# A hybrid streaming-encoder step: a margin in the planner that orders TensorE, and two groups of loads asked for at other places

## The chip, the cores and the metric

One NeuronCore of one Trainium2 chip runs the whole step. The metric is the device time of one execution in microseconds, lower is better. A kernel is timed in several executions and the median is compared; one further execution is recorded by the hardware profiler, and every row quoted below comes from that one.

## The reference

One layer of an encoder is computed in float32 for a prompt of 1024 frames and a sample of 64 frames that share the weights (width 1024). Cut to what matters:

```python
h = rms_norm(xp, g_norm1)
qa, ka, va, qb, kb, vb, logf = in_proj(h, w_in, ...)     # h @ w_in, 8 + 8 heads of 64
oa = chunk_band_attn_prompt(qa, ka, va, rel_bias)        # 64-frame chunks, 8 chunks back
ob = forget_attn_prompt(qb, kb, vb, logf)                # causal, bias from cumsum(logf)
xp = xp + concat([oa, ob]) @ w_o
mk, mv = mem_kv(mem_prompt, g_mem, w_mkv, g_mk)          # 256 memory tokens @ (1024 x 2048)
xp = xp + mem_attend(rms_norm(xp, g_norm2), mk, mv, w_mq, g_mq, w_mo)
xp = xp + conv_ffn(rms_norm(xp, g_norm3), ..., w_up, w_conv, b_conv, w_down)
# the sample does the same with cached keys and values (1024 past rows for the causal heads,
# 512 for the banded ones) in place of a mask, and with a cached memory
```

Projected keys and values, the memory's keys and values, log-forget values and the last conv rows are outputs too.

## The kernel before, in words

Products run on TensorE (PE) with each float32 operand split into a high and a low fp32r part; three products (high-high, low-high, high-low) give one. ScalarE (ACT) makes the high part by a cast, VectorE (DVE) or GpSimd (POOL) the low part by a subtraction. All DMAs are issued by SyncE (SP), one after another, each behind the semaphores it waits for.

The program has these stages in order of time:

- **Opening** (to about 62 us in the profile): the first projection starts with four 128-frame blocks at once while weights and frames arrive. It ends with the product of the 64 sample frames (L535), which needs the sample's columns split into two parts (GpSimd L205, ScalarE L210, VectorE L211 `xs`).
- **Eight head pairs** (about 62 to 530 us): for each pair the projection (L413, tile `pj`) of nine blocks is woven with the attention of the pair's finished blocks. Every two blocks, TensorE turns queries and keys (L484, tile `tq`), ScalarE and VectorE split them into `q` and `k` (L488 to L495). A score group (L706, tile `S`, one buffer of two banks) needs `q` (VectorE L495) and the buffer, which the group before gives back when VectorE has added the bias and taken the extreme (L709, `mx`). Behind it come the exponential on ScalarE (L711), the scaling on GpSimd (L713), the turning of the probabilities (TensorE L743, tile `PT`), their split (L744, L745) and the value product (L762, tile `O`).
- **Memory keys and values, with the sample's attention woven in** (about 530 to 622 us): 16 units (n = 0 to 7, t = 0, 1) of 24 products each (L829) use weights that arrive raw in two halves of 512 KB (`mwraw`, issued by L813 in `load_wm`) and are split in four quarters (L821 `mwhi` on ScalarE, L822 `mwlo` on VectorE, in `split_wm`). Raw and split tiles share eight places each under two tags. `mem_end` (L955 to L958) normalises a unit's keys, `mem_turn` (L977) turns them. Meanwhile eight sample units (`Sample`: `load` issues its queries, keys and values at L996 to L1005, `load_bias` its bias at L1014 or L1016, then `prep`, `score` L1045, `turn` L1069, `sum` L1083, `out`).
- **Output projection, memory attention, feed-forward** (to the end): L1183, then L1739 and L2063.

Up to the instruction count `arranged` the traced order is only the priority. `arrange` re-plans it: it gives each traced instruction its dependencies, a duration from a table of costs (`cost`), and plays the five engines forward. At each step the engine that can start first takes, among its instructions whose predicted inputs are there, the one traced first. The order that comes out is pinned by dependencies between neighbours on each engine. Hardware then runs each engine's list in order, so an instruction whose input is later than predicted holds up all that is planned behind it. A DMA may not start, in the plan, before the product traced ten places ahead of it has begun (`AHEAD`); otherwise SP follows the same rule, with traced order as priority. Behind `arranged` the traced order stands as written.

Of the kernel before, what the change touches and what calls it, by code (L numbers as in the profile page):

```python
# [41 lines left out]
def hybrid_step(ctx: ExitStack, tc: tile.TileContext, i: dict, o: dict):  # L42
# [768 lines left out]
    def load_wm(n, z):  # L811
        raw = raw_of[n, z] = quarter_tile(QUARTERS[z], "mwraw", F32)
        nc.sync.dma_start(raw.rearrange("p k c -> p (k c)"), i["w_mkv"][n, z])  # L813
# [122 lines left out]
    kvs, stores, waiting = {}, [], []  # L936
# [162 lines left out]
    for u, (n, t) in enumerate(units):  # L1099
        for c in range(4):  # L1100
            def piece(n=n, t=t, c=c, u=u):
                if n < 7 and t == 1:
                    split_wm(n + 1, c)
                if n in range(1, 6) and t == 0 and c in (1, 2):
                    load_wm(n + 2, c - 1)
                mem_piece(n, t, c)
                if c == 1:
                    flush(0)
                if c == 2 and u:
                    mem_turn(*units[u - 1])  # L1110
                if c == 3:
                    mem_end(n, t)
            line.append(piece)
# [16 lines left out]
    samples = [Sample(p) for p in SAMPLES]  # L1130
# [134 lines left out]
    for x in range(len(samples) + 1):  # L1265
        if not line and ha is None:
            ha, split, early_x = open_left()
            left_at = x
        cur = samples[x] if x < len(samples) else None
        nxt = samples[x + 1] if x + 1 < len(samples) else None  # L1270
        if nxt:
            nxt.load_bias()
        if x + 3 < len(samples):
            samples[x + 3].load()
        if x in (5, 6):
            load_early(x - 5)
        new, fin = [], []
        if cur:
            new = [cur.score]
        if nxt:  # L1280
            fin = [nxt.prep]
        subs = new[:1] + old[:2] + new[1:] + old[2:-1] + fin[:1] + old[-1:] + fin[1:]
        main = line[:PER[x]]
        del line[:PER[x]]
        if ha and x == left_at:
            pieces = first[0].pieces
            subs = new[:1] + old[:2] + split[0][:1] + new[1:] + split[0][1:2]
            subs += [lambda: stream.upto(1)] + old[2:-1] + split[0][2:4] + [lambda: stream.upto(2)]
            subs += [pieces[0], split[0][4], pieces[1], split[0][5]] + old[-1:] + [pieces[2], split[0][6], pieces[3], split[0][7]]
        elif ha:  # L1290
            main = pieces[4:] + [f for two in zip(split[1], first[1].pieces) for f in two]
            subs = [lambda: stream.upto(4)] + subs
        weave(main, subs)
        if cur:
            c = cur.nc
            old = [lambda z=z, u=cur: u.turn(z) for z in range(2)] + [lambda u=cur: u.sum(0)]
            old += ([lambda u=cur: u.turn(2), lambda u=cur: u.sum(1)] if c == 2 else [])
            old += [lambda u=cur, c=c: u.sum(c), cur.out]
# [243 lines left out]
    for n, u in enumerate(mems):  # L1542
        h, c = u.h, u.c
# [69 lines left out]
    for w, m in enumerate(ROWS):  # L1613
        x = long_row("qhi")
# [472 lines left out]
def arrange(tc, end):  # L2087

    import heapq

    signal = 0.07
    nodes, owner, made, touched, opened, closed = [], {}, {}, {}, {}, []
    writer, readers, group = {}, {}, {}
    setter = select = None
# [161 lines left out]
    while True:  # L2256
        start, engine = min((earliest(e), e) for e in ENGINES)
        if start == 1e9:
            break
        while coming[engine] and coming[engine][0][0] <= start:  # L2260
            n = heapq.heappop(coming[engine])[1]
            heapq.heappush(waiting[engine][nodes[n][6]], n)
        a, b = waiting[engine]
        line = min([x for x in (a, b if port <= start else []) if x], default=None)
        if line is None:
            continue
        n = heapq.heappop(line)
        order[engine].append(n)
        _, _, _, _, busy, done, shared = nodes[n]
        free[engine] = start + busy  # L2270
        if engine == "SP":
            lane = max(lane, start + 1.4) + done
            done = lane - start + 0.3 + min(0.5, done / 2)
        if shared:
            port = start + busy
        for t in held[n][1]:
            if t not in taken:
                taken.add(t)
                slots[owner[t][2]].remove(min(slots[owner[t][2]]))
            left[t] -= 1  # L2280
            over[t] = max(over[t], start + done + signal)
            if not left[t]:
                slots[owner[t][2]].append(over[t])
                for m in stuck.pop(owner[t][2], ()):
                    release(m)
        for m, begun in after[n]:
            same = nodes[m][1] == engine
            ready[m] = max(ready[m], start + (0 if begun else busy if same and engine == "PE" else done if same and engine != "SP" else done + signal))
            missing[m] -= 1
            if not missing[m]:  # L2290
                release(m)
# [91 lines left out]
```

## Time and profile before

| | |
|---|---|
| runs | 1693.71, 1690.34, 1694.01 us; median 1693.71 |
| profiled execution | 1686.39 us, its span 1684.6 us |
| instructions | 33070, of them 12027 matmuls |
| busy share of the span | TensorE 99%, its weight loads 96%, VectorE 69%, ScalarE 54%, GpSimd 35% |
| DMA | 199.82 MB at a mean of 119 GB/s |

The profiler's row of a matmul has a start that is recorded and an end that is modelled from the size; matmuls overlap in it. Two equal products start 0.17 to 0.18 us apart at 384 columns though each row lasts 0.34 us. A pause of up to about 0.2 us between two of them therefore leaves TensorE busy without a break. Weight loads (PEld) have rows of their own, and their pauses show earlier. The times of 1.8 us outside the span belong to start and end of the execution.

### The profile page before, as it was taken

How to read it: one execution, taken by the hardware profiler on the slowest of the kernel's cores; microseconds unless marked ns; L12 is line 12 of the kernel's file. 1: busy time of each engine (PE TensorE's matmuls, PEld its weight loads, DVE VectorE, ACT ScalarE, POOL GpSimd, SP SyncE). 2: the span in 40 equal slices, each digit the busy share in tenths (PEclk: the TensorE clock that was granted, in tenths of full speed). 3: DMA queues.
4: the chain of work that ended last, by engine and by line, in shares of the span. 5: the costliest groups of instructions: out<-in, count | busy, mean ns of one | idle time of the engine just before them, and what ended most of it. 6: DMA issues, size and time to landing. Idle time of an engine off the chain costs nothing.

```text
span 1684.6 us, 33070 instructions
## 1 busy us (share of the span) xinstructions
PE 1660.5 (99%) x12027; PEld 1613.2 (96%) x12027; DVE 1166.4 (69%) x2584; ACT 907.9 (54%) x2003; POOL 583.2 (35%) x846
## 2 busy tenths in 40 slices
PE   9999999999999999999999999999999999999999
PEld 8899899999998879999999999999999999999999
DVE  7866866766778644344553797777777777559996
ACT  8866677767777564345555554333333333444442
POOL 1756688888853213444446111000000000000000
PEclk9999999999999999999999999999999999999999
DMA  7323243232235974421115632222222222983332
GB/s 242 91 77 84 76 113 91 77 92 84 64 118 165 290 216 152 141 82 58 55 58 162 214 115 84 77 78 77 78 77 77 78 78 84 320 298 120 102 109 88
DMA packets 142260, 199.82 MB, mean 119 GB/s; under 512 B 22200, under 2 KB 85304, under 8 KB 142096
## 3 DMA queue, kind: packets, MB, share of 16 engines
q1 hardware_dynamic: 142096, 197.70, 37.8%
q8 instruction: 95, 1.56, 0.4%
q14 instruction: 69, 0.57, 0.1%
HBM read 148.01 MB, written 43.34 MB: 114 GB/s over the span
## 4 chain that ended last, share of the span: by engine, by line
PE 87%; ACT 4%; DVE 4%; DMA 2%; issue 1%; SPq 0%; POOL 0%; DVEq 0%; ACTq 0%; POOLq 0%
PE W L1739 27%; PE W L2063 14%; PE pj L1183 14%; PE pj L413 11%; PE S L706 4%; PE O L762 3%; PE PT L743 3%; PE pj L829 2%; PE W L1183 1%; PE pj L535 1%; PE S L1475 1%; PE tq L1514 1%; PE O L1514 1%; PE tq L484 1%; DMA k<-k 1%
## 5 line engine op out<-in xcount | busy, mean ns | idle before, releaser
L413 PE MATMUL pj<-whi,xhi 128*128 128x384 f32 (+1 forms) x480 | 172.7, 360 | 0.0
L413 PE MATMUL pj<-whi,xlo 128*128 128x384 f32 (+1 forms) x480 | 164.7, 343 | 0.0
L413 PE MATMUL pj<-wlo,xhi 128*128 128x384 f32 (+1 forms) x480 | 164.1, 342 | 0.0
L1739 PE MATMUL W<-h,hi 128*128 128x272 f32 x704 | 134.3, 288 | 1.4 <-ACT qlo L1875 1.4
L1845 POOL COPY s<-gp 128x2 f32<-128x2 f32 x22 | 15.8, 719 | 336.1 <-DVE gp L1844 336.1
L2063 PE MATMUL W<-f,hi 128*128 128x272 f32 x672 | 127.2, 287 | 0.0
L745 DVE TENSOR_TENSOR ptl<-PT,pth 128x512 fp32r<-128x512 f32 (+2 forms) x192 | 97.9, 521 | 32.4 <-ACT pth L744 30.6
L713 POOL TENSOR_SCALAR s<-s,ssum 128x640 f32<-128x640 f32 (+7 forms) x128 | 92.9, 728 | 68.2 <-DVE ssum L712 52.2
L711 ACT ACTIVATE s<-s,mx 128x640 f32<-128x640 f32 (+7 forms) x128 | 94.5, 738 | 35.9 <-DVE mx L709 35.0
L744 ACT CAST pth<-PT 128x512 fp32r<-128x512 f32 (+2 forms) x192 | 84.6, 451 | 54.1 <-PE PT L743 52.4
L1739 PEld LDWEIGHTS W<-h,hi 128*128 128x128 f32 x704 | 110.3, 188 | 1.7 <-ACT qlo L1875 1.6
L2063 PEld LDWEIGHTS W<-f,hi 128*128 128x128 f32 x672 | 105.2, 188 | 0.1
L1739 PE MATMUL W<-h,lo 128*128 128x272 f32 x352 | 101.3, 288 | 0.0
L706 PE MATMUL S<-k,q 128*128 128x256 f32 (+3 forms) x432 | 90.5, 323 | 7.2 <-DVE mx L709 2.8
L2063 PE MATMUL W<-f,lo 128*128 128x272 f32 x336 | 96.7, 288 | 0.0
L1602 ACT CAST hi<-raw 128x512 fp32r<-128x512 f32 x68 | 42.2, 621 | 98.7 <-PE W L1739 59.2
L413 PEld LDWEIGHTS pj<-whi,xhi 128*128 128x128 f32 x480 | 90.6, 189 | 1.5
L413 PEld LDWEIGHTS pj<-wlo,xhi 128*128 128x128 f32 x480 | 90.8, 189 | 0.7
L413 PEld LDWEIGHTS pj<-whi,xlo 128*128 128x128 f32 x480 | 90.3, 188 | 0.4
L743 PE MATMUL PT<-ident,s 128*128 128x128 f32 x528 | 87.6, 273 | 0.8 <-DVE ptl L745 0.8
L706 PEld LDWEIGHTS S<-k,q 128*128 128x128 f32 x432 | 67.3, 188 | 21.8 <-DVE q L495 8.1
L1183 PE MATMUL pj<-a,hi 128*128 128x384 f32 (+1 forms) x352 | 87.2, 332 | 1.0 <-DVE a L1236 0.9
(611 smaller groups left out, 5684.3 us busy)
## 6 DMA issues: line engine op xcount, KB each, us to landing
raw<-in_w_down_dram SPq DMA_DIRECT2D x45, 256.0 KB, 2.7
wraw<-in_w_dram SPq DMA_DIRECT2D x56, 192.0 KB, 2.7
raw<-in_w_up_dram SPq DMA_DIRECT2D x41, 256.0 KB, 2.7
h<-ad SPq DMA_DIRECT2D x32, 272.0 KB, 5.1
mwraw<-in_w_mkv_dram SPq DMA_DIRECT2D x16, 512.0 KB, 5.6
raw<-in_w_mo_dram SPq DMA_DIRECT2D x32, 256.0 KB, 3.2
kvraw<-in_w_down_dram SPq DMA_DIRECT2D x32, 256.0 KB, 3.4
k<-k SPq DMA_DIRECT2D x60, 128.0 KB, 2.4
```

What stands on the lines that cost most here:

```text
L413: pe.matmul(pj[:, :nw], x_part(a, k, t * P, P), wt[k][b][:, :nw], start=n == 0, stop=n == 3 * KT - 1)
L706: pe.matmul(sp[:, a:a + m], q, ring[:, h, z, k0:k0 + m], start=z == 0, stop=z == 1)
L711: act.activation(s[:, :n], s[:, :n], ACT.Exp, bias=mx, scale=-1.0, accum_out=sm)
L713: pool.tensor_scalar(s[:, :n], s[:, :n], sm, 1.0, op0=ALU.mult, op1=ALU.mult)
L743: pe.transpose(pt[:, b - ch[0]], self.s[j][:, (b - w0) * P:(b - w0 + 1) * P], ident)
L744: act.copy(hi[:, f:f + n, j], pt[:, f:f + n])
L745: dve.tensor_tensor(lo[:, f:f + n, j], pt[:, f:f + n], f32(hi[:, f:f + n, j]), op=ALU.subtract)
L762: pe.matmul(op[:r, cols], v[:, :r], self.pts[b][m][:, x, cols], start=first and (b, m) == steps[0], stop=ch[-1] == self.last and (b, m) == ...
L1183: pe.matmul(out()[:, :cn], w[a][:, k % 4], x[b][k][:, c0:c0 + cn], start=k == 0 and (a, b) == SPLIT[0], stop=k == KT - 1 and (a, b) == SPL ...
L1602: act.copy(hi, t)
L1739: pe.matmul(w[:, z, :Q], a(p, j), rights[j][b][:, z * Q:z * Q + Q], start=fresh and begin and j == 0 and x == 0, stop=final and end and j ...
L2063: pe.matmul(ws[m][:, z, :Q], la[p][:, m * P:(m + 1) * P], ra[b][:, z * Q:z * Q + Q], start=first and y == 0 and what in opening, stop=fina ...
```

## The change

Three edits, and no instruction is added or removed: each engine has the same number of instructions of each kind before and after.

1. In `arrange`, TensorE takes an instruction only if its inputs were predicted to be there 0.2 us ago, as long as another one waits that satisfies this. If none does, the first to come is taken as before. A product that depends only on an earlier TensorE instruction is marked ready 0.2 us early, so that the margin is nil for a chain on TensorE itself.
2. The loads of sample x+3 are traced behind the work that is woven in iteration x, and not ahead of it, so they have a lower priority among SP's instructions.
3. The raw memory weights of n+3 are traced in unit (n, 1), right behind the splits that end the use of a raw half of n+1; before, those of n+2 were traced in unit (n, 0), three pieces later.

```diff
             def piece(n=n, t=t, c=c, u=u):
                 if n < 7 and t == 1:
                     split_wm(n + 1, c)
-                if n in range(1, 6) and t == 0 and c in (1, 2):
-                    load_wm(n + 2, c - 1)
+                if n < 5 and t == 1 and c in (2, 3):
+                    load_wm(n + 3, c - 2)
                 mem_piece(n, t, c)
...
         if nxt:
             nxt.load_bias()
-        if x + 3 < len(samples):
-            samples[x + 3].load()
         if x in (5, 6):
             load_early(x - 5)
...
         weave(main, subs)
+        if x + 3 < len(samples):
+            samples[x + 3].load()
         if cur:
...
-    signal = 0.07
+    signal, sure = 0.07, {"PE": 0.2}
...
-        while coming[engine] and coming[engine][0][0] <= start:
+        a, b = waiting[engine]
+        while coming[engine] and coming[engine][0][0] <= start - (sure.get(engine, 0.0) if a or b else 0.0):
             n = heapq.heappop(coming[engine])[1]
             heapq.heappush(waiting[engine][nodes[n][6]], n)
-        a, b = waiting[engine]
...
         for m, begun in after[n]:
             same = nodes[m][1] == engine
-            ready[m] = max(ready[m], start + (0 if begun else busy if same and engine == "PE" else done if same and engine != "SP" else done + signal))
+            ready[m] = max(ready[m], start + (0 if begun else busy - sure[engine] if same and engine == "PE" else done if same and engine != "SP" else done + signal))
```

What the planner makes of it is seen in the lists of the engines. The first place is **TensorE in the head pairs**, between two score groups of one query group (`S_4650` and `S_4702`, both with `q_4612`). Before:

```order
L706 MATMUL S_4650<-k_416,q_4612 128x384 x2
L413 MATMUL pj_4641<-whi_4063,xlo_396 128x384
L743 MATMUL PT_4714<-ident_61,s_4582 128x128 x2
L413 MATMUL pj_4641<-whi_4075,xhi_395 128x384
L413 MATMUL pj_4641<-wlo_4076,xhi_395 128x384
L413 MATMUL pj_4641<-whi_4075,xlo_396 128x384
L413 MATMUL pj_4641<-whi_4111,xhi_395 128x384
L706 MATMUL S_4702<-k_416,q_4612 128x512 x2
```

The same two groups in the changed kernel:

```order
L706 MATMUL S_4650<-k_416,q_4612 128x384 x2
L413 MATMUL pj_4641<-wlo_4076,xhi_395 128x384
L413 MATMUL pj_4641<-whi_4075,xlo_396 128x384
L413 MATMUL pj_4641<-whi_4111,xhi_395 128x384
L413 MATMUL pj_4641<-wlo_4112,xhi_395 128x384
L413 MATMUL pj_4641<-whi_4111,xlo_396 128x384
L413 MATMUL pj_4739<-whi_3579,xhi_515 128x384
L413 MATMUL pj_4739<-wlo_3580,xhi_515 128x384
L413 MATMUL pj_4739<-whi_3579,xlo_516 128x384
L413 MATMUL pj_4739<-whi_3692,xhi_515 128x384
L706 MATMUL S_4702<-k_416,q_4612 128x512 x2
```

Five projection products and two turns stood between the groups; now nine projection products do, and the two turns stand ahead of the first group. Along the whole list turns are broken up more: of the transposes on TensorE up to the output projection, 324 runs ended in a product before and 412 do now, since a single turn and a single product often alternate.

The second place is **SP around the last two halves of raw memory weights** (`mwraw`; L964 and L965 store memory values, L1014 is a sample's bias, L996 to L1005 are a sample's loads). Before:

```order
L964 DMA out_mv_dram<-kv 128x256
L965 DMA vmd<-kv 128x256
L1014 DMA s<-rows 64x576 x2
L996 DMA sqd<-sqk 64x256
L998 DMA svn<-sv 64x128
L1001 DMA kraw<-in_cak_dram 64x512 x2
L1005 DMA vraw<-in_cav_dram 128x512
L813 DMA mwraw<-in_w_mkv_dram 128x1024
L964 DMA out_mv_dram<-kv 128x256
L965 DMA vmd<-kv 128x256
L813 DMA mwraw<-in_w_mkv_dram 128x1024
```

And now:

```order
L964 DMA out_mv_dram<-kv 128x256
L965 DMA vmd<-kv 128x256
L813 DMA mwraw<-in_w_mkv_dram 128x1024 x2
L996 DMA sqd<-sqk 64x256
L998 DMA svn<-sv 64x128
L1001 DMA kraw<-in_cak_dram 64x512 x2
L1005 DMA vraw<-in_cav_dram 128x512
L1014 DMA s<-rows 64x576 x2
```

The two halves stood behind a sample's seven loads and one or two pairs of stores; they now stand right behind the first pair of stores, ahead of those loads. Halves before them stand earlier too.

The third place is **VectorE at the end of the opening**, around the split of the sample's columns (`xs`, L211; L709 is the evacuation of a score group). Before:

```order
L709 ISA s,mx<-S,bias 128x640
L709 ISA mx 128x1
L458 CAST v<-vf 128x2x64
L709 ISA s,mx<-S,bias 128x640
L709 ISA mx 128x1
L712 RECIPROCAL ssum<-ssum 128x1
L771 TENSOR_TENSOR mix<-O,otmp 64x256
L211 TENSOR_TENSOR xs<-s,xs 128x8x64
```

And now:

```order
L709 ISA s,mx<-S,bias 128x640
L709 ISA mx 128x1
L211 TENSOR_TENSOR xs<-s,xs 128x8x64
L451 SCALAR_TENSOR_TENSOR flog<-qkraw,rstd_81,bfb 128x8
L712 RECIPROCAL ssum<-ssum 128x1
L709 ISA s,mx<-S,bias 128x640
```

The split stands right behind the first of these score groups and ahead of the second. On ScalarE the cast for it (L210) has moved ahead of the exponential of the first group, and on TensorE the third score group has moved behind the sample product L535.

## The prediction, made before the changed kernel ran

> **What bounds the kernel now.** I read the page first, then windows of 100 us, then waits, and last the timeline around the longest ones. The page gives the span and the engines' busy time:
>
> ```profile
> span 1684.6 us, 33070 instructions
> PE 1660.5 (99%) x12027; PEld 1613.2 (96%) x12027; DVE 1166.4 (69%) x2584; ACT 907.9 (54%) x2003; POOL 583.2 (35%) x846
> ```
>
> TensorE sets the time, and the 99% leaves 24.1 us. But matmul rows overlap, so short pauses are invisible in it; weight loads show more of them. Windows (span of the window, then busy time of PE, PEld, DVE, ACT, POOL, the granted clock, DMA share, GB/s):
>
> ```profile
> 300.00:400.00 100.00, 99.52 (x650) 94.06 (x650) 71.88 (x190) 72.76 (x180) 87.65 (x141) 1.00 0.29 81
> 1100.00:1200.00 100.00, 100.00 (x801) 100.00 (x799) 76.38 (x131) 38.04 (x56) 7.00 (x17) 1.00 0.26 84
> 550.00:560.00 10.00, 8.26 (x59) 7.07 (x58) 8.88 (x27) 6.96 (x20) 3.21 (x8) 1.00 1.03 320
> ...
> 592.00:596.00 4.00, 4.00 (x17) 3.46 (x18) 1.58 (x3) 2.40 (x8) 0.00 (x0) 0.57 0.53 145
> ```
>
> The feed-forward has no pause at all, and no instruction there moves. In the head pairs the weight loads miss 6% of the time. The memory stage has real holes, DMA that is full, and once four microseconds at a mean clock of 0.57. The change can therefore give or take only in the first 625 us. Waits of weight loads between 62 and 500 us, and of matmuls in the whole span (total us, times, longest):
>
> ```profile
> PEld S L706 <- DVE q L495: 7.6, 22, 0.8
> PEld S L706 <- DVE mx L709: 3.7, 7, 0.7
> ...
> PE S L706 <- DMA k<-k: 2.6, 3, 2.1
> PE PT L977 <- DVE kv L958: 1.7, 1, 1.7
> PE O L1083 <- ACT pth L1073: 1.5, 1, 1.5
> ```
>
> The head pairs lose little bits at score groups. The memory stage loses three longer pieces, and they are the longest of the whole region.
>
> **A: the last raw weights.** The last of these three waits reads like this (start, length, engine, line, and in brackets the idle time and its releaser):
>
> ```profile
> 590.57 0.48 PE L1083 MATMUL O<-svn,pth 64*128 64x128 f32 x2 [1.52 <-ACT pth L1073]
> 589.38 0.62 ACT L821 CAST mwhi<-mwraw 128x512 fp32r<-128x512 f32 x1 [3.29 <-DMA mwraw<-in_w_mkv_dram]
> 589.91 0.47 ACT L961 ACTIVATE kv<-pj,rmem 128x256 f32<-128x256 f32 x1
> 590.28 0.24 ACT L1073 COPY pth<-PT 64x128 f32<-64x128 f32 x1
> 577.58 1.32 SPq L964 DMA_DIRECT2D out_mv_dram<-kv  x1
> 578.95 0.43 SPq L965 DMA_DIRECT2D vmd<-kv  x1
> 584.85 0.38 SPq L813 DMA_DIRECT2D mwraw<-in_w_mkv_dram  x1
> 586.30 0.43 SPq L813 DMA_DIRECT2D mwraw<-in_w_mkv_dram  x1
> ```
>
> ScalarE sat 3.29 us for a raw half, `pth` stood behind that cast, and TensorE behind `pth`. The half asked for at 586.30 was cast at 589.38, 3.1 us later. In the new list of SP both halves stand right behind L964 and L965, so they can be asked for at about 579.4, 5.5 and 6.5 us earlier: more than ScalarE's 3.29. The pause of 1.52 goes. The row of 592 to 596 lies 1.4 us behind it and loses 4.00 x (1 − 0.57) = 1.7 us to the clock; I count it as a consequence. A = −(1.5 + 1.7) = **−3.2**, bounds −3.2 and 0. What is late next: the sample loads (L996 to L1005) and bias pair that now come behind the weights.
>
> The clock is the place where I weigh a rule. Two longer pauses, 1.7 and 2.1 us, were followed by a clock of 1.00 (550 to 560 above; 530 to 540 below), and the one of 1.52 by the half clock.
>
> ```profile
> 530.00:540.00 10.00, 10.00 (x86) 9.79 (x85) 8.44 (x29) 7.03 (x22) 3.20 (x4) 1.00 0.85 239
> ```
>
> The Trainium skill, page "TensorE: Matmul & The Clock Gate", section 1 on what is actually happening, says that the clock falls to one half after an idle window of about 3.4 us. By that rule a pause of 1.52 us does not cause it, and A would be 1.5 alone; the trace agrees on the two longer pauses, and shows nothing of the kind for the third.
>
> **B: keys of the memory at 555 us.**
>
> ```profile
> 553.66 1.23 DVE L1048 CUSTOM_DVE_ANT_0 s<-S,s 128x1024 f32<-128x1024 f32 x1 [0.17 <-issue]
> 554.81 0.48 DVE L958 SCALAR_TENSOR_TENSOR kv<-pj,mr,gmk 128x256 f32<-128x256 f32 x1
> 555.44 0.41 PE L977 MATMUL PT<-ident,kv 128*128 128x128 f32 x2 [1.74 <-DVE kv L958]
> ```
>
> VectorE took the sample's scores (1.23 us) ahead of the `kv` that TensorE waited for. In the new order `kv` stands ahead of L1048, since the low parts of weights are made earlier. That takes 1.23 of the 1.74 away; bounds −1.7 (all), and +1.0, if L1048, which gives the score buffer back, then holds TensorE for most of its 1.23. I take **−1.0**, near the gain, because the row names the culprit.
>
> **C: the margin in the head pairs.** At the place shown in the lists above (`S_4702`):
>
> ```profile
> 299.15 0.34 PE L413 MATMUL pj<-whi,xlo 128*128 128x384 f32 x1
> 299.32 0.33 PE L413 MATMUL pj<-whi,xhi 128*128 128x384 f32 x1
> 300.05 0.50 PE L706 MATMUL S<-k,q 128*128 128x512 f32 x1 [0.39 <-DVE mx L709]
> ```
>
> Products start 0.17 to 0.18 us apart; the score group started 0.73 after the last, so 0.55 was lost, though the row admits 0.39. Now nine products stand between instead of five and two turns: 9 x 0.175 = 1.6 us against 5 x 0.175 + 2 x 0.11 = 1.1. That covers the 0.55 almost fully. It costs nothing as long as the products put ahead would have run behind anyway, which is the cover: 435 x 3 products of L413 in this stretch. What is deferred is the score group itself, and behind it L709, the exponential, the scaling and L743.
>
> The 29 waits above add to 7.6 + 3.7 = 11.3 us, 0.39 each. One product more ahead of each of them, 0.175 us, less where the wait was shorter: 29 x 0.145 = 4.2. The best end is three quarters of 11.3, −8.4, if two or three products ahead, as at `S_4702`, were typical; the worst is +2, if the deferred groups only move the wait one link down the chain (VectorE 72% and GpSimd 88% busy from 300 to 400). I take **−4.2**, the one-product value, as the margin asks for 0.2 us and no more.
>
> **D: end of the opening.**
>
> ```profile
> 55.34 1.04 POOL L205 TENSOR_TENSOR s<-s,gcol 128x512 f32<-128x512 f32 x1
> 57.14 0.60 ACT L210 CAST xs<-s 128x512 fp32r<-128x512 f32 x1
> 58.36 0.87 PE L706 MATMUL S<-k,q 128*128 128x384 f32 x4 [1.03 <-DVE mx L709]
> 58.86 1.03 DVE L211 TENSOR_TENSOR xs<-s,xs 128x512 fp32r<-128x512 f32 x1
> 60.04 0.42 PE L535 MATMUL pj<-whi,xs 128*128 128x392 f32 x1 [0.81 <-DVE ms L179]
> 56.00:62.00 6.00, 4.15 (x26) 3.76 (x25) 4.61 (x16) 5.34 (x15) 5.68 (x8) 1.00 0.58 162
> ```
>
> The last row is a window: 1.85 us idle in six. The cast may now start at 56.38 where GpSimd ends, and the low part at 57.0 instead of 58.86; so L535 can fill the pause 1.0 us ahead of the third score group. That group (the row of 0.87) then runs behind L535 and no longer covers the split; of its 0.87 I count 0.65, an estimate, as cover lost. I take 1.85 − 0.65 = **−1.2**; bounds −1.9 (all of the idle time) and +1.0 (one more wait like that of 1.03).
>
> **E, F, G: smaller ones.** The 2.1 us for `k<-k`, a DMA whose place on SP stays, get some five products of L829 more ahead, 0.12 each: bound −0.6, and +1.7 if a pause there is the next to bring the half clock. I take **−0.3**. **F:** turns are broken up more. Four turns and a product against one and one:
>
> ```profile
> 334.13 0.60 PE L743 MATMUL PT<-ident,s 128*128 128x128 f32 x4
> ...
> 334.75 0.34 PE L413 MATMUL pj<-wlo,xhi 128*128 128x384 f32 x1
> 343.12 0.27 PE L743 MATMUL PT<-ident,s 128*128 128x128 f32 x1
> ...
> 343.40 0.34 PE L413 MATMUL pj<-wlo,xhi 128*128 128x384 f32 x1
> ```
>
> From the first turn to the second product 334.75 − 334.13 = 0.62, and 343.40 − 343.12 = 0.28: three turns more are 0.34, 0.113 each, so a lone turn with its product costs 0.28 against 0.113 + 0.175 = 0.288. Splitting is free within the rounding of these rows, some 7 ns of either sign. There are 412 − 324 = 88 more runs, so the bounds are −0.6 and +0.6; I take **+0.4**, toward a loss, which is a choice and not a row. **G:** a wait that is not there now, most likely for a sample's late loads or bias. The slack of one bias today is
>
> ```profile
> 576.23 1.23 POOL L1031 TENSOR_SCALAR s<-s,stok 128x1088 f32<-128x1088 f32 x1 [5.51 <-DMA s<-negs]
> 577.53 0.52 POOL L1034 TENSOR_SCALAR_AFFINE_SELECT s<-s 64x64 f32<-64x64 f32 x2
> 582.66 1.23 DVE L1048 CUSTOM_DVE_ANT_0 s<-S,s 128x1024 f32<-128x1024 f32 x1 [2.60 <-PE S L1045]
> ```
>
> 582.66 − 578.05 = 4.6 us, which seven loads at 0.38 to 0.43 us of SP (L813 above), about 3 us, fit into. Bounds 0 and +3.2 (one more case like A); I take **+1.0**.
>
> **Sum:** −3.2 − 1.0 − 4.2 − 1.2 − 0.3 + 0.4 + 1.0 = −8.5 us; span 1676.1, profiled execution 1686.39 − 8.5 = 1677.9. The median of the runs lies 7.3 above the profiled execution; I carry the same difference over: 1693.71 − 8.5 = **1685.2 us**.
>
> **Rivals.**
> 1. *Half clock is not the pause's doing.* For it: two longer pauses with a clock of 1.00. Against: the four slow microseconds follow the pause by 1.4 us and in windows of 20 us over the whole span no other has a clock below 1.00. A is then 1.5: −6.8, 1686.9.
> 2. *The margin does nothing.* The waits in the head pairs are 0.39 long in the mean, and where inputs come 0.5 late, 0.2 may only move the pause. C = 0: −4.3, 1689.4.
> 3. *Memory is the bound in the memory stage.* A DMA share of 1.03 from 550 to 560 speaks for it: what goes first pushes something else back, A and B stay, G is 2: −3.3, 1690.4. Against: the windows of 592 to 596 and 530 to 540 (0.53, 0.85) show room. With rival 2 on top: +0.9, 1694.6.
> 4. *Slower: deferral isn't covered.* Every one of the 124 score groups
>
> ```profile
> L709 DVE DVE_READ_ACCUMULATOR2_ANT mx<- 128x1 f32 x124 | 10.2, 83 | 0.0
> ```
>
> may be put behind other work for 0.2 us though its inputs were in time. Their chain (L709, exponential, GpSimd at 88%, L743) sets the end where projection work has run out, as at the end of a pair and from 500 to 530. With 0.08 us of each uncovered C is +10: −8.5 + 4.2 + 10 = +5.7, 1699.4. It decides from the point where C passes +4.3, 0.035 us a group. Against: from 300 to 400 us GpSimd still has 12% free, ScalarE 27%.
>
> **How the numbers follow.** Chances: forecast 0.44, rival 1 0.08, rival 2 0.12, rival 3 0.12, 2 and 3 together 0.08, rival 4 0.16. A measurement of this kernel can tell about 0.2%, 3.4 us, from no change. Forecast and rival 1 are faster; rivals 2 and 3 lie on the edge at −4.3 and −3.3, half of their 0.24 counts as faster: 0.44 + 0.08 + 0.12 = **0.64**; the same is 0.12 + 0.08 = **0.20**; slower **0.16**. The best ends add to −16.4 (−3.2 − 1.7 − 8.4 − 1.9 − 0.6 − 0.6), 1677.3; so the range begins at **1677**. Upward it takes rivals 1 to 3 in and half of rival 4: **1697**. The forecast's own range is 1681 to 1690.
>
> **What would show it.** A: no wait of L821 for `mwraw` near 589, no idle ahead of L1083, and a clock of 1.00 from 590 to 600; with rival 1 the slow window stays. B: L977 waits under 0.7. C: the 11.3 us of weight-load waits fall to about 7, and the busy share of weight loads from 300 to 400 rises above 94%; unchanged waits are rival 2, a later end of the eighth pair rival 4. D: L535 starts 1 us earlier. G: no new wait above 1 us for a sample's load or bias. The prediction is wrong if the pauses that vanish come back under other names within the same stage, so that TensorE enters the output projection at the same time as before.

## The result and the profile after

The changed kernel takes 1682.52 us in the median (1679.71 to 1685.26), the kernel before on the same chip 1693.45 (1688.96 to 1695.15): a ratio of 0.9939, interval 0.9921 to 0.9956, or 10.9 us less. On a second chip it was 1680.73 against 1689.22, a ratio of 0.9950 (0.9933 to 0.9968), 8.5 us less. The prediction was 1685.2, 8.5 us less, with a range of 1677 to 1697.

The page of the changed kernel (span; busy time of the engines):

```profile
span 1677.9 us, 33051 instructions
PE 1655.4 (99%) x12027; PEld 1614.7 (96%) x12027; DVE 1159.6 (69%) x2584; ACT 907.1 (54%) x2003; POOL 583.0 (35%) x846
```

Every engine has the same number of counted instructions as before; the 19 fewer in all are of kinds that do not count as busy. The profiled execution took 1679.75 us, 6.6 less than that of before. Where these went is read off four starts in the two traces: of the first sample product (L535), the first memory product (L829), the first product of the output projection (L1183), and the end of the span.

| stage (us) | before | changed | difference | predicted |
|---|---|---|---|---|
| start to first L535 (opening) | 60.0 | 57.4 | −2.6 | D −1.2 |
| first L535 to first L829 (head pairs) | 459.9 | 455.0 | −4.9 | C, F −3.8 |
| first L829 to first L1183 (memory stage) | 101.4 | 102.1 | +0.7 | A, B, E, G −3.5 |
| first L1183 to the end | 1063.3 | 1063.4 | +0.1 | 0 |

So the gain sits ahead of 512 us, and the memory stage, which was to give two fifths of it, gave nothing. The first three starts are marks that move with the order: four score products (L706) that ran ahead of the first L535 now run behind it, and two turns and five value products that ran ahead of the first L829 now run behind it. For the head pairs the two shifts nearly cancel; the opening's −2.6 is read again below. In the head pairs the waits of weight loads between 62 and 500 us are these, in the changed kernel:

```profile
PEld S L706 <- DVE q L495: 2.6, 9, 0.4
PEld S L706 <- DVE mx L709: 2.0, 3, 1.0
PEld PT L743 <- DVE ptl L745: 1.9, 4, 0.9
PEld PT L743 <- POOL s L713: 0.8, 1, 0.8
```

The waits of score groups fell from 11.3 to 4.6 us and from 29 to 12 in number. Some came back one link further down the chain: the turns of the probabilities (L743) now wait 1.9 us for their low part, 0.5 before. All waits of weight loads in this window add to 11.1 us, 15.3 before. Windows of before (first) and of the changed kernel, with the columns of the prediction's windows:

```profile
50.00:62.00 12.00, 8.59 (x56) 7.55 (x55) 10.02 (x28) 9.93 (x25) 11.25 (x15) 1.00 0.59 149
62.00:500.00 438.00, 434.19 (x2874) 410.33 (x2873) 314.68 (x874) 308.46 (x792) 331.43 (x519) 1.00 0.31 85
```

```profile
50.00:62.00 12.00, 10.02 (x65) 8.97 (x63) 10.35 (x29) 10.09 (x26) 9.87 (x14) 1.00 0.58 157
62.00:500.00 438.00, 433.95 (x2902) 415.63 (x2901) 316.29 (x883) 312.22 (x802) 335.75 (x525) 1.00 0.32 88
```

From 62 to 500 us the matmul rows are busy for the same time, though 28 more of them run in it (28 x 0.175 = 4.9 us); the weight loads, 410.3 to 415.6, show the gain. In the opening it is plain in both. Its end now reads:

```profile
54.87 0.62 ACT L210 CAST xs<-s 128x512 fp32r<-128x512 f32 x1
56.10 1.22 DVE L211 TENSOR_TENSOR xs<-s,xs 128x512 fp32r<-128x512 f32 x1
57.37 0.44 PE L535 MATMUL pj<-whi,xs 128*128 128x392 f32 x1
```

In the memory stage the waits of matmuls between 500 and 640 us are:

```profile
PE S L1045 <- ACT sq L1027: 2.4, 2, 1.8
PE PT L977 <- DVE ptl L1071: 1.3, 1, 1.3
PE pj L1183 <- DVE a L1236: 1.2, 2, 0.9
PE PT L977 <- DVE kv L958: 0.9, 1, 0.9
PE S L706 <- DMA k<-k: 0.9, 1, 0.9
```

The 1.5 us ahead of L1083 and its wait for raw weights are gone, `kv` costs 0.9 in place of 1.7, and `k` 0.9 in place of 2.1. Two pauses stand there that were not there before, and each can be followed back in the timeline:

```profile
531.80 1.14 ACT L821 CAST mwhi<-mwraw 128x512 fp32r<-128x512 f32 x2
532.84 0.58 ACT L744 CAST pth<-PT 128x512 fp32r<-128x512 f32 x1
533.45 0.37 ACT L770 COPY otmp<-O 64x256 f32<-64x256 f32 x1
533.95 0.31 ACT L1027 ACTIVATE sq<-tq,gd 64x64 f32<-64x64 f32 x1
534.74 1.16 PE L1045 MATMUL S<-kraw,sq 128*128 128x512 f32 x2 [1.77 <-ACT sq L1027]
...
550.22 0.47 SPq L1016 DMA_DIRECT2D s<-negs  x1
557.83 1.19 POOL L1031 TENSOR_SCALAR s<-s,stok 128x1088 f32<-128x1088 f32 x1 [5.24 <-DMA s<-negs]
559.05 1.22 DVE L1048 CUSTOM_DVE_ANT_0 s<-S,s 128x1024 f32<-128x1024 f32 x1 [2.90 <-POOL s L1031]
561.02 0.68 DVE L1071 COPY ptl<-PT 128x512 f32<-128x512 f32 x1
561.76 0.44 PE L977 MATMUL PT<-ident,kv 128*128 128x128 f32 x2 [1.32 <-DVE ptl L1071]
```

The first: TensorE waits for the sample's scaled queries, and they stand on ScalarE behind two casts of weights (1.14 us) and other work. The first such product also stands earlier in TensorE's order than before: it ran at 544.93 in the kernel before. What of the 1.77 us the casts make, and what the earlier place, no run separates. The second: the half bias that SP asked for at 550.22 was used by GpSimd at 557.83, 7.6 us later; VectorE waited 2.90 us for GpSimd, and the copy that TensorE needs stood behind it. In the kernel before, the bias for this sample was asked for at 552.58 and used 7.2 us later, and VectorE waited for it already:

```profile
559.73 1.76 POOL L1031 TENSOR_SCALAR s<-s,stok 128x1088 f32<-128x1088 f32 x1 [5.39 <-DMA s<-negs]
561.52 1.22 DVE L1048 CUSTOM_DVE_ANT_0 s<-S,s 128x1024 f32<-128x1024 f32 x1 [0.88 <-POOL s L1031]
```

So it had no slack, and it is asked for later now: its first half 5.1 us ahead of the sample's score product (549.08 to 554.14), 6.6 us before (552.58 to 559.22). And the clock fell behind the first pause (the window's columns: busy time of TensorE, granted clock, DMA share, GB/s):

```profile
536.00:540.00 4.00, 4.00 (x25) 0.61 0.55 167
```

4 x 0.39 = 1.6 us. So 1.77 + 1.32 + 1.6 = 4.7 us of new losses in the place of what A, B and E took away (3.2 + 0.8 + 1.2 = 5.2). That sums to −0.5, and the stage took 0.7 more; the 1.2 us between them are not traced.

### The profile page after: what moved, and what is told of

Its sections match the earlier page's. It is cut to its first block, busy times and chain, and to the rows that moved or that the text cites. A ratio compares the mean times of both kernels' runs of the same rounds, so it can differ in the third digit from the quotient of the medians.

```text
span 1677.9 us, 33051 instructions
## 1 busy us (share of the span) xinstructions
PE 1655.4 (99%) x12027; PEld 1614.7 (96%) x12027; DVE 1159.6 (69%) x2584; ACT 907.1 (54%) x2003; POOL 583.0 (35%) x846
## 4 chain that ended last, share of the span: by engine, by line
PE 84%; ACT 5%; DVE 5%; DMA 3%; issue 2%; SPq 1%; POOL 0%; DVEq 0%; ACTq 0%; POOLq 0%
PE W L1739 27%; PE W L2063 14%; PE pj L1183 13%; PE pj L413 10%; PE S L706 3%; PE O L762 3%; PE PT L743 3%; PE pj L829 2%; PE pj L535 1%; PE S L1475 1%; PE W L1183 1%; PE tq L1514 1%; PE O L1514 1%; DMA k<-k 1%; DMA wraw<-in_w_dram 1%
## 5 line engine op out<-in xcount | busy, mean ns | idle before, releaser
L743 PE MATMUL PT<-ident,s 128*128 128x128 f32 x528 | 96.2, 275 | 2.2 <-DVE ptl L745 1.3
L706 PE MATMUL S<-k,q 128*128 128x256 f32 (+3 forms) x432 | 91.6, 320 | 3.2 <-DMA k<-k 1.1
L1183 PE MATMUL pj<-a,hi 128*128 128x384 f32 (+1 forms) x352 | 83.8, 330 | 1.5 <-DVE a L1236 1.2
L706 PEld LDWEIGHTS S<-k,q 128*128 128x128 f32 x432 | 69.9, 188 | 12.0 <-DVE q L495 3.6
```

Of the source, the lines that this page charges most:

```text
L706: pe.matmul(sp[:, a:a + m], q, ring[:, h, z, k0:k0 + m], start=z == 0, stop=z == 1)
L743: pe.transpose(pt[:, b - ch[0]], self.s[j][:, (b - w0) * P:(b - w0 + 1) * P], ident)
L1183: pe.matmul(out()[:, :cn], w[a][:, k % 4], x[b][k][:, c0:c0 + cn], start=k == 0 and (a, b) == SPLIT[0], stop=k == KT - 1 and (a, b) == SPL ...
```

## The experiments

My theory after this was: the margin gives the gain, since the planner takes inputs to be ready earlier than they are; in the memory stage a transfer that goes first pushes another back, as DMA is full there. Against it stood that the moved loads matter, and that any new order of thousands of instructions would do as much.

**One part at a time.** The margin alone (all of `arrange`'s edits, both groups of loads as before):

```diff
-                if n < 5 and t == 1 and c in (2, 3):
-                    load_wm(n + 3, c - 2)
+                if n in range(1, 6) and t == 0 and c in (1, 2):
+                    load_wm(n + 2, c - 1)
...
+        if x + 3 < len(samples):
+            samples[x + 3].load()
...
         weave(main, subs)
-        if x + 3 < len(samples):
-            samples[x + 3].load()
```

> Only edit 1, the margin of 0.2 us for TensorE in the planner; both groups of loads stay where they were. Theory (the margin puts work ahead of late inputs): most of the gain is here, 7 to 9 us less than before, and the weight-load waits of score groups for q and mx between 62 and 500 us fall from 11.3 us to about 5, as they did with the whole change. Rival 'moved loads': the margin is worth little and this is within 3 us of before. Rival 'any new order' (planning again just draws another order of the same worth): a difference of either sign, and waits of about 11 us.

Ratio 0.9967 (0.9955 to 0.9979), which of 1689.17 us is 5.6 less: most of the gain, though less than the 7 to 9 put down. The first L829 starts at 512.3, as with the whole change (512.4), and the waits are the same too:

```profile
PEld S L706 <- DVE q L495: 2.7, 9, 0.4
PEld PT L743 <- DVE ptl L745: 2.1, 5, 0.9
PEld S L706 <- DVE mx L709: 2.1, 3, 1.0
```

In this profile the memory stage took 101.8 us with the loads at their old places, against 102.1 and 104.2 in the two profiles of the whole change (the second is shown below). So with this margin no profile shows that the moved loads gained there. The pause ahead of L1083 was 0.8 us here with a clock of 1.00 behind it: the margin alone took half of that pause and its half clock away. The two new pauses, ahead of L1045 near 535 and of L977 behind the bias, are not there.

The loads alone (`arrange` as before):

```diff
-    signal, sure = 0.07, {"PE": 0.2}
+    signal = 0.07
...
-        while coming[engine] and coming[engine][0][0] <= start - (sure.get(engine, 0.0) if a or b else 0.0):
+        while coming[engine] and coming[engine][0][0] <= start:
...
-            ... busy - sure[engine] if same and engine == "PE" ...
+            ... busy if same and engine == "PE" ...
```

> Only edits 2 and 3, both groups of loads moved and no margin. Theory: 1 to 3 us less than before, all of it in the memory stage (530 to 625 us), weight-load waits of the head pairs unchanged at about 11 us. Rival 'moved loads': 7 us or more less than before. If the two parts add up, this one and the margin alone give the 10.9 us of the whole change between them.

Ratio 0.9987 (0.9976 to 0.9999), about 2 us less. The waits of the head pairs are those of before, 7.7 and 3.7 us:

```profile
PEld S L706 <- DVE q L495: 7.7, 22, 0.8
PEld S L706 <- DVE mx L709: 3.7, 7, 0.7
```

The product of the two ratios is 0.9954, inside both intervals of the whole change. But the gain of the loads is not where I expected it: in the profiled execution the memory stage took 102.9 us, with a new pause of 3.4 us ahead of L977 and half clock behind it, so this profile does not show where the 2 us are won. At that pause VectorE waited 4.85 us for GpSimd and its bias. That wait was 0.88 before, is absent with the margin alone, and is 2.90 us with both: the late bias comes with the moved loads.

**The size of the margin.** Each of these is the whole change with another number:

```diff
-    signal, sure = 0.07, {"PE": 0.2}
+    signal, sure = 0.07, {"PE": 0.1}
```

> The whole change with a margin of 0.1 us in place of 0.2. Theory: inputs come late by up to 0.8 us and 0.39 in the mean, so half the margin covers about half: 3 to 5 us slower than with 0.2, waits for q and mx in the head pairs between 5 and 11 us. Rival 'any new order': no trend with the size of the margin.

> The whole change with a margin of 0.4 us in place of 0.2. Theory: waits for q and mx in the head pairs fall to 1 to 3 us, 1 to 3 us faster than with 0.2. Rival 'deferral': score groups start later by another 0.2 us and the chain behind them ends later; waits of the turns (L743) for the low part ptl grow, and it is 2 to 5 us slower than with 0.2. Rival 'any new order': no trend.

> The whole change with a margin of 0.6 us. So far the stretch from the sample product L535 to the first memory product L829 took 459.9 us before, 459.5 with 0.1, 455.0 with 0.2 and 449.2 with 0.4. Theory (the planner's predicted input times are too early by up to 0.8 us, a larger margin covers more of them): about 447, waits for q and mx between 62 and 500 us under 3 us, time within 3 us of that with 0.4 or better. Rival 'deferral' (score groups pushed back too far, the chain behind them ends later): over 452, and slower than with 0.4 by 3 us or more. Rival 'any new order': no trend, anything between 449 and 460.

> The whole change with a margin of 0.8 us. L535 to L829 took 459.5, 455.0, 449.2 and 447.3 us with 0.1, 0.2, 0.4 and 0.6. Theory: the longest of the waits it covers were 0.8 us and few are left, so the curve is flat here, 446 to 449. Rival 'deferral': 450 or more, as score groups are pushed back further than their inputs are late.

| margin (us) | ratio to before (interval) | first L535 | L535 to L829 | L829 to L1183 | waits for q and mx |
|---|---|---|---|---|---|
| none (loads moved) | 0.9987 (0.9976 to 0.9999) | 59.8 | 459.2 | 102.9 | 11.4 |
| 0.1 | 0.9990 (0.9978 to 1.0001) | 57.2 | 459.5 | 100.6 | 7.3 |
| 0.2 | 0.9939 (0.9921 to 0.9956) | 57.4 | 455.0 | 102.1 | 4.6 |
| 0.4 | 0.9935 (0.9923 to 0.9947) | 59.9 | 449.2 | 102.0 | 3.6 |
| 0.6 | 0.9905 (0.9884 to 0.9925) | 58.2 | 447.3 | 104.3 | 2.4 |
| 0.8 | 0.9950 (0.9933 to 0.9968) | 61.0 | 445.7 | 110.7 | 1.3 |

By these starts the head pairs follow the margin, by up to 13.5 us. But the larger margins also push work past the mark: behind the first L829 there ran 20 score products and 32 turns with 0.4, 28 and 40 with 0.6, 36 and 40 and eight more value products with 0.8. That is some 2 and 4 us of work, and it is all that 0.6 and 0.8 seem to gain over 0.4. It is an estimate from the distance of starts in the traces, 0.14 us for a score product, 0.12 for a value product and 0.11 for a turn. A fixed window says the same: from 62 to 500 us TensorE ran 2874 matmuls before, and 2868, 2902, 2927, 2931 and 2923 with the five margins. So the curve is flat from 0.4 on, and its worth there is some 9 us, an estimate: 53 matmuls more than before, of 0.175 us each.

The margin of 0.1 took waits for `q` and `mx` away without making the stretch shorter, which is not the half that I expected. All waits of weight loads from 62 to 500 us fit this: 15.3 us before and 15.4 with 0.1, then 11.1, 6.4, 4.9 and 4.5. With 0.1 what score groups no longer waited came back at other products. With 0.4 the waits for `q` and `mx` were 3.6 us, and not the 1 to 3 expected. With 0.6 the waits for `q` have left the list, and these are its first two rows:

```profile
PEld S L706 <- DVE mx L709: 2.4, 3, 1.2
PEld O L762 <- ACT pth L744: 1.0, 3, 0.5
```

'Deferral' makes nothing slower in the head pairs; it shows behind them, as the work that 0.6 and 0.8 push into the memory stage: the last value product (L762) starts at 536.7, 536.4 and 544.9 us with 0.4, 0.6 and 0.8. In time, 0.2 and 0.4 can't be told apart. The time does not follow the stretch because other stages give some of it back: with 0.4 TensorE had run 329 matmuls by 62 us, with 0.2 it was 337; with 0.8 it was 313, as half clock fell into the opening, and the memory stage was 8.6 us longer, with one pause of 4.5 us and half clock around it. The lowest ratio of all kernels run is that with 0.6: 1673.62 us against 1689.79 of before.

**Is it the margin or only a new order?** No margin, moved loads, and another time for a signal:

```diff
-    signal, sure = 0.07, {"PE": 0.2}
+    signal = 0.09
```

> Both groups of loads moved and no margin, but the planner's time for a signal between engines is 0.09 us in place of 0.07, which draws another order of thousands of instructions. Theory: a new order by itself is worth nothing; L535 to L829 within 2 us of 459.2 (moved loads alone), waits for q and mx 10 to 12 us, time within 3 us of moved loads alone. Rival 'any new order': this one differs by 5 us or more, of either sign, and the margins have only been lucky draws.

Ratio 0.9985 (0.9968 to 1.0001), the same as the moved loads alone (0.9987); L535 to L829 457.1, 2.1 us less. So this other order was worth 2.1 us in the stretch, a little over the 2 expected and half of what the margin of 0.2 gives there; it is one draw and bounds nothing. What speaks against 'any new order' in the head pairs is the trend besides: every kernel with a margin of 0.2 or more took 456.2 us or less in the stretch, every other one 457.1 or more. The waits for `q` and `mx` were 3.7 and 3.7 us here, not 10 to 12, while all waits of weight loads add to 13.7 (15.3 before): those two alone are a sign of the loss, not its measure.

**The broken-up turns.** Marking chains earlier by a hair keeps turns together:

```diff
-            ... busy - sure[engine] if same ...
+            ... busy - sure[engine] - 1e-6 if same ...
```

> The whole change, with chains on TensorE marked ready a millionth of a microsecond earlier still, so that the rounding of sums no longer makes the planner pass over a turn whose predecessor has just been issued: the turns (L743) stay together as before the change, and the margin of 0.2 stays. Theory: breaking up turns costs next to nothing (0.4 us was put down for it), so within 2 us of the whole change, L535 to L829 at 454 to 456. Rival: the broken-up turns cost several us, or are themselves what helps by spreading the work of ScalarE and VectorE; then it differs by 3 us or more.

Ratio 0.9956 (0.9940 to 0.9971), where the whole change had 0.9939 and 0.9950; L535 to L829 454.7 against 455.0. In the stretch where the turns are, breaking them up cost nothing that shows. The profiled execution itself was 5 to 7 us longer than the two of the whole change, from the opening (60.1) and the memory stage (105.9, with a pause of 6.4 us ahead of L977 near 555 and half clock around it). The order is another one in these stages too, so this says nothing about turns outside the head pairs.

**What holds the memory stage.** First, 2 MB less for the DMA; this kernel leaves out the second half of the cached keys and values of the four causal sample units:

```diff
-            self.k = self.pl.tile([P, self.ctx], F32, name="kraw", bufs=3 if self.early else 4)
+            self.k = self.pl.tile([P, 512], F32, name="kraw", bufs=3 if self.early else 4)
             for h in range(2):
-                nc.sync.dma_start(self.k[h * S:h * S + S], self.ck[2 * (p % 4) + h, 0:S])
+                nc.sync.dma_start(self.k[h * S:h * S + S], self.ck[2 * (p % 4) + h, 0:S, 0:512])
-            self.v = []
-            for c in range(self.nc):
-                raw = ...
-                self.loaded = nc.sync.dma_start(..., self.cv[p % 4, c])
-                self.v.append(raw)
+            raw = ...
+            self.loaded = nc.sync.dma_start(..., self.cv[p % 4, 0])
+            self.v = [raw] * self.nc
...
-                pe.matmul(sp[:, c], q, self.k[:, c * 512:(c + 1) * 512], start=True, stop=True)
+                pe.matmul(sp[:, c], q, self.k[:, 0:512], start=True, stop=True)
```

> The whole change, but the four causal samples load only the first half of their cached keys and values and use it twice, so that the sample's attention is computed from the wrong half there: 2 MB less for the DMA engines between about 520 and 560 us, and the same work on every other engine. Theory (the memory stage is held up by DMA that is full, so a load that is asked for earlier only pushes back another): its pauses fall by half or more, and the stage from the first L829 to the first L1183 gets 2 to 4 us shorter than the 102.1 us of the whole change; what 2 MB take at 290 GB/s is 7 us. Rival (the order of ScalarE and VectorE makes the pauses, whatever the DMA does): the stage stays within 1 us of 102.

Ratio 0.9920 (0.9896 to 0.9945). The stage took 99.0 us, 3.1 less than in the first profile of the whole change and 5.2 less than in the second, and its two new pauses are down to these (its lines stand one lower, so L1044 is L1045 and L1070 is L1071):

```profile
PE S L1044 <- ACT sq L1026: 0.7, 1, 0.7
PE PT L977 <- DVE kv L958: 0.6, 1, 0.6
PE PT L977 <- DVE ptl L1070: 0.5, 1, 0.5
```

It is the shortest stage of all kernels run (the next is 100.6, with the margin of 0.1), which points to the bytes. It is not proof: the edit also takes four requests from SP and lets the planner draw another order, and it is one profile. Does it matter, then, which is first? Two kernels with the margin of 0.6, one with both groups of loads back at the old places (the diff of the margin alone, with 0.6), one with the third sample later:

```diff
-    ahead = [[samples[0].load], [samples[1].load], [samples[0].load_bias, samples[2].load], [samples[0].prep]]
+    ahead = [[samples[0].load], [samples[1].load], [samples[0].load_bias], [samples[0].prep]]
...
+        if x == 0:
+            samples[2].load()
```

> A margin of 0.6 us with both groups of loads where they were before the change. Theory (DMA is full between 530 and 590 us whatever is asked for first): the moved loads are worth nothing with this margin; L535 to L829 at 447 to 449, the memory stage within 2 us of the 104.3 that it takes with the moved loads, time within 3 us of margin_06. Rival: the moved loads carry 2 us or more, and this is slower by as much, with a wait for raw weights ahead of L1083 back.

> A margin of 0.6 us, and the loads of the third sample are traced at the start of the first woven iteration, so that three halves of raw weights come ahead of them on SP; no byte is added or removed. Theory (with DMA full, what matters is which transfer is first, and the raw weights hold ScalarE, VectorE and TensorE, while the third sample is needed some 25 us later): the pause of 3.5 us ahead of L1022 near 543 and its half clock go, and the memory stage takes 100 to 102 us in place of 104.3; 2 to 4 us faster than margin_06. Rival: the pause turns up elsewhere with the same length, or the third sample is late itself; 104 us or more.

Old places: ratio 0.9942 (0.9924 to 0.9961) against 0.9905 with the loads moved, on another chip; the two intervals meet only at their ends. The stage takes 109.5 us against 104.3, and A's chain is back, longer than before:

```profile
583.33 0.62 ACT L821 CAST mwhi<-mwraw 128x512 fp32r<-128x512 f32 x1 [4.00 <-DMA mwraw<-in_w_mkv_dram]
584.52 0.49 PE L1083 MATMUL O<-svn,pth 64*128 64x128 f32 x2 [2.20 <-ACT pth L1073]
```

Of the 5.2 us more in the stage 2.2 are this pause; a pause of 3.0 us ahead of L977, with longer half clock, also stands where the moved loads have 3.5 us ahead of L1022. So my expectation that the moved loads are worth nothing fell, and the rival named there holds. That they matter more, the earlier TensorE reaches the stage, is a guess from two margins. The third sample later: ratio 0.9914 (0.9894 to 0.9934), stage 106.0 and not the 100 to 102 expected; the pause ahead of L1022 went from 3.5 to 2.0 us and kept its half clock, and others of 1.1 us each came ahead of L977 and L1083. There the rival holds too. Fewer bytes went with a shorter stage; of two orders of the same bytes one helped and one did not.

**The whole change again,** unchanged:

> The whole change once more, as it is, on the same chip as the next three and with a second profile. Theory: the pauses are the order's and come back at the same instructions with lengths within 0.3 us (1.8 us ahead of L1045, 1.3 ahead of L977 near 562), and the time is 0.5 to 0.8% below before. Whether the half clock behind the pause of 1.8 us comes back is open: if it follows from the pause alone, it does; if it depends on where the pause falls in time, it may not. Stage from L829 to L1183 then 102.1 or about 100.4 us.

The time fits (0.9950). The two pauses come back at the same instructions, the first with the same length, the second not:

```profile
536.37 1.12 PE L1045 MATMUL S<-kraw,sq 128*128 128x512 f32 x2 [1.77 <-ACT sq L1027]
564.69 0.44 PE L977 MATMUL PT<-ident,kv 128*128 128x128 f32 x2 [2.97 <-DVE ptl L1071]
538.00:542.00 4.00, 4.00 (x37) 1.00 0.39 123
564.00:568.00 4.00, 3.31 (x26) 1.00 1.00 278
```

The clock did not fall behind either. The stage took 104.2 us, 2.1 more than in the first profile although it lost no clock, and L535 to L829 456.2, 1.2 more.

## Why the prediction was right, and where not

**The total** is right: −8.5 was forecast, −10.9 and −8.5 were measured on two chips. The way there is only half right, and in part the hit is luck: the profiled executions, from which the terms were worked out, differ by 6.6 us and, with the second profile, by 4.4. The sign of being wrong that the prediction named came true by half: pauses that vanished came back under other names within the memory stage, but TensorE entered the output projection 6.8 us earlier (3.4 in the second profile), since the head pairs and the opening gave more than forecast.

**C** is right in kind and size. C and F together were −3.8 and gave −4.9 (−3.7 in the second profile), most of it from the margin alone. The one-product value was the right choice between the bounds for 0.2; the best end of three quarters needs a margin of 0.4 or more. That waits are the mechanism is borne out: all waits of weight loads fell from 15.3 to 11.1 us, about as much as the stretch. Rivals 2 and 4 fall for this change: 0.2 is enough to move the stretch and does not lengthen it. Deferred work appears with 0.6 and 0.8, and ends up in the memory stage.

**D** had the right sign and was too small. The −2.6 by the start of L535 flatters it, as the third score group had moved behind that start. At a fixed time it reads: by 62 us the changed kernel had run 11 more projection products and two more turns, 11 x 0.175 + 2 x 0.11 = 2.1 us (1.9 in the second profile), about at the bound of −1.9. The idle time from 56 to 62 us went from 1.85 to 0.14, so the 0.65 counted as cover lost was the term that failed. The cast's earliest start was wrong too: I let it begin when GpSimd ends at 56.38 as before, but in the new order it ran at 54.87.

**E** was −0.3 with a bound of −0.6, and the wait for `k` fell by 1.2 (0.9 in the repeat). The five products of L829 that I counted do stand ahead of it now (34 against 29), and with them four value products and a turn that I had not counted.

**F** is right: with the turns kept together the head pairs take the same time.

**A** is right in its chain and wrong in its worth. The wait for raw weights and the pause ahead of L1083 went away, and came back, with 2.2 us, when the loads were put back under the larger margin. But 1.7 of its 3.2 us was the half clock, and the repeat shows that this doesn't follow from a pause alone. With the margin alone, 0.7 us of the pause and the half clock were gone as well, so beside this margin the moved loads had only 0.8 us left to take.

**B** is right in size: −0.8 against −1.0. Which part brings it is open: with each part alone the wait was 1.6 and 1.8 us, and with the moved loads and the other signal time it was 0.9.

**G** is the term that was mis-sized: +1.0 with a bound of +3.2. It measured +4.7 in the first profile. The late bias that it named is one of its two parts. The step that failed there is the slack: I read 4.6 us at the bias used at 576.23, and took it for all of them. The bias that came late had none; VectorE waited 0.88 us for it before the change already, so every later request on SP counted. The other part, queries behind weight casts on ScalarE, I had not seen: I asked what comes late when weights come first on SP, and not what else stands on ScalarE ahead of a product that TensorE reaches earlier. This is rival 3 in effect, with A and B taken and given back; at a tenth to a fifth I gave it too little.

**The carried difference** between the profiled execution and the median covered this miss. By profiles the gain was 6.6 us, by medians 10.9. The profiled execution of before was 7.3 us below the median of its first three runs; that of the change 2.8 below its own, and the second 1.3 above. A single execution can be a lucky one by some microseconds. No profile shows where the other executions of before lose that time, but their granted clocks say what it goes with: of 23 executions of before on one chip, the two with a mean clock of 1.000 took 1684.4 and 1686.3 us, the three with 0.996 took 1691.9 to 1694.2. Four thousandths of 1685 us are 6.7 us, most of that distance. The profiled execution had 0.999. I carried the whole difference over as if the change could not touch it.

## What to carry to other kernels

Where a planner fixes the order of in-order engines, inputs that are predicted a little too early cost a pause each time; let the bound engine prefer work whose inputs have been there for a while, and choose the size by trying it: here 0.1 gave nothing in the stretch, 0.4 twice what 0.2 gave, and more than 0.4 only moved work into the next stage. When stages are measured from the start of one product to that of another, count what crosses these marks. A transfer that is moved ahead in a stage whose DMA is full pushes others back: look for slack at each of those, not at one, and follow what is pushed back on the engines as well as on the issuing queue. And a sum that is made on one profiled execution is worth a second profile: here the same kernel differed by 2 us in one stage.

## What the runs showed of the hardware

The granted clock falls to half behind pauses much shorter than the slow stretch itself, and not each time. In the kernel before a pause of 1.52 us was followed by four microseconds at a mean of 0.57, which is 3.4 us at one half. The same pause of 1.77 us ahead of L1045 was followed by a clock of 0.61 over four microseconds in one execution, and of 1.00 in another. Around 50 us two kernels have nearly the same idle time (TensorE busy 0.91 and 0.92 us from 49 to 51, 1.32 in both from 51 to 53). With the third sample later (first) and with the plain margin of 0.6 the next two microseconds read:

```profile
53.00:55.00 2.00, 1.54 (x8) 0.50 0.69 196
```

```profile
53.00:55.00 2.00, 1.30 (x12) 1.00 0.69 210
```

Over all profiles and behind the first 20 us, seven of the eight pauses of TensorE of 2.9 us or more had half clock (0.50) within 8 us, and of the seventeen from 1.3 to 2.2 us four had it, the 1.52 of before and the 1.77 of the change among them. The Trainium skill, page "TensorE: Matmul & The Clock Gate", section "What's actually happening", describes a window of about 3.4 us that runs freely, so that the moment of a change depends on where in it the work falls; that the same pause has different consequences agrees with it. Its rule that the clock falls after an idle window of that length does not by itself cover the pause of 1.52, after which no whole 3.4 us were idle; here the measurement decides.
